# Second MLP product of a decoder layer: operands made ahead in other buffers, the last convolution moved behind them, the residual added by DMA

## The chip, the cores and the metric

One core of a Trainium2 chip runs the whole layer in one launch. The metric is the device time of one execution in microseconds (us). The engines are TensorE (PE, its weight loads PEld), VectorE (DVE), ScalarE (ACT), GpSimd (POOL) and SyncE (SP), which only issues DMAs here.

## The reference, cut to what matters

A hybrid decoder layer (state-space mixer, windowed attention, then a gated MLP) over 1024 positions with 1024 channels, all in float32. The change lies in the last part:

```
up = h @ w_up                                   # 1024 x 5632
up = causal depthwise conv of width 3 (up) + conv_b
val, gate = split(up, 2)                        # 2816 each
x = x + g2 * ((silu(gate) * val) @ w_down)      # second MLP product, then the residual
```

## The kernel before, in words

Everything is held transposed: channels on the partitions, positions along the free axis. The first MLP product makes `up` in 22 tiles f of 128 value and 128 gate channels. Each tile is one 2 by 2 block product done in seven products i = 1 to 7 instead of eight, with sums of operands taken before and of results after. A float32 operand is cut into a high part (fp32r) and the rest (`split`, L137: the high part by ACT through `cpy`, L133, the low part by a subtraction, L118, on DVE or POOL), and `mm3` (L143) makes three matmuls of each pair. After its seven products a tile f has its value half `uv[f]` (buffer H6 or A8) and its gate half `ug[f]` (buffer H7), taken out of PSUM by `took` (L1039). Then `conv` (L1099) runs over the gate into buffer X7 (one ACT instruction at L1100, two DVE instructions at L127), the SiLU follows on ACT, `conv` runs over the value into X6, DVE multiplies both, and SP stores the product to DRAM as `gd[f]` (L1200).

The second MLP product contracts over the 22 tiles, in 11 pairs p cut into three chunks of 3, 4 and 4 pairs (L1153). Again seven products i, in the order 1, 5, 6, 3, 7, 2, 4. A step is one (chunk, i, p), 77 in all, and has 12 matmuls of 128x512. `fetch(p)` loads four tiles of 512 KB (two of `gd`, two of `w_down`) into the buffers `homes[p]`. `operands(i, p)` does up to three DVE subtractions or additions in place (three for i = 5, two for 6, one for 3, 7 and 4), and then two `mixed` calls, each of which takes the next buffer of `SLOTS` and splits the operand into it. `mix_next` does this for the next step in the list; inside the loop it stays three steps ahead (AH, L1223). `put` (L1162) scales a finished bank of PSUM by g2 into the output tile `xo[k]`: by ACT the first time a half tile is written, by DVE (L127) after that.

The operand buffers of the steps come from a cycle of nine: U0, U1, U4, U5, U2, U3, A8, H7, H6. U0 to U5 hold the last weights of the first product, H7 and H6 the last tile's two halves, so step 3 (buffers A8, H7) waits for the last gate convolution and step 4 (H6, U0) for the last value convolution. In the program the last tile's convolutions (f = 21, L1192 to L1200) stand ahead of all but the first two steps' operands.

The residual lies in DRAM as `xd`. At steps 21 and 30 SP loads its eight tiles into H4, H5, X4, X5 (L1231 to L1234), and at eight of the steps 24 to 36 DVE adds a whole 128x1024 tile to `xo[k]` (L1235 to L1237).

The order of the instructions on each engine and queue is laid down when the kernel is built, by a planner that takes the program's order as priority and a simulated timeline for what is ready (L1361). An engine works through its queue in that order. An adding DMA is used once before in this kernel: in `proj` POOL issues 16 of them, 256 KB each (L888), to add the layer's input.

Of the kernel before, what the change touches and what calls it, by code (L numbers as in the profile page):

```python
# [22 lines left out]
FFT = 22  # L23
# [39 lines left out]
def hymba_kernel(ctx, tc, xT, c, wmod, wu, wkvq, small, consts, relb, pq, wglu, wout, wup, wdn, out):  # L63
# [1047 lines left out]
    cn_ = {"slot": 0, "split": 0}  # L1111
# [12 lines left out]
    def mixed(v):  # L1124
        r_ = half(newr(SLOTS[cn_["slot"] % len(SLOTS)]))
        cn_["slot"] += 1
        split(r_, v, "a", "vvp"[cn_["split"] % 3])
        cn_["split"] += 1
        return r_

    SLOTS = ("U0", "U1", "U4", "U5", "U2", "U3", "A8", "H7", "H6")
# [43 lines left out]


# [7 lines left out]
    for n_, (f, i) in enumerate(seq):  # L1184
# [7 lines left out]
        if i == 4:  # L1192
            tg = new("X7")
            conv(tg, FFT + f, ug[f])
            act.activation(out=tg, in_=tg, func=AF.Silu)
        elif i == 3:
            tv = new("X6")
            conv(tv, f, uv[f])
            tt(vec, tv, tv, tg, MUL)
            kept = sync.dma_start(out=gd[f], in_=tv)  # L1200
            if f == 3:
                cact4 = new("H4")
                sync.dma_start(out=cact4, in_=cad.partition_broadcast(128))
            elif 4 <= f < 12:
                with tc.issue_after(kept.ins):
                    emit_mod(36 + f, new("H5"), cact4)
        if f == FFT - 2 and i == 3:
            fetch(0)
            fetch(1)
        if f == FFT - 1 and i == 5:  # L1210
            fetch(2)
        if f == FFT - 1 and i in (4, 3):
            mix_next()
# [3 lines left out]
    xo = [xq[:, k * 1024:(k + 1) * 1024] for k in range(4)] + [new(t_) for t_ in ("W0", "W1", "X6", "X7")]  # L1217
    fetch_at = {5: 3, 8: 4, 12: 5, 16: 6, 24: 7, 28: 8, 33: 9, 46: 10}
    XL = {21: (0, 1, 2, 3), 30: (4, 5, 6, 7)}
    XP = {24: 0, 25: 1, 26: 2, 27: 3, 33: 4, 34: 5, 35: 6, 36: 7}  # L1220
    xt, pend, touched, banks = {}, None, set(), {}
    np_ = 0
    AH = 3  # L1223
    for s_, (c_, i, p) in enumerate(steps):
# [3 lines left out]
        if s_ in fetch_at:  # L1228
            with tc.issue_after(kept.ins):
                fetch(fetch_at[s_])  # L1230
        if s_ in XL:  # L1231
            for k in XL[s_]:
                xt[k] = new(("H4", "H5", "X4", "X5")[k % 4])
                sync.dma_start(out=xt[k], in_=xd[k])  # L1234
        if s_ in XP:  # L1235
            k = XP[s_]
            tt(vec, xo[k], xo[k], xt[k], ADD)  # L1237
# [16 lines left out]
        if p == ps_[1] and pend:  # L1254
            put(*pend)
        if p == ps_[-1]:
# [108 lines left out]
```

## Time and profile before

| | |
|---|---|
| median of 3 runs | 1137.26 us (1137.13 to 1140.05) |
| profiled execution, its own time | 1138.01 us |
| its span, first to last instruction | 1136.1 us |
| mean granted TensorE clock | 0.962 |
| busy: PE, DVE, ACT, POOL | 1050.8, 928.0, 581.0, 269.0 us |
| PE at lines of the chain that ended last | 44% of the span |
| second MLP product, from the first step alone on PE to the end | 903.7 to 1132.4 us |

The profiled execution is 0.75 us longer than the median, and 1.9 us of it lie outside the span. A busy PE says little here, since it is busy in nearly all of the span; what can be changed is seen in the places where it is idle or runs at a lower granted clock (1.00 is 2.4 GHz, 0.50 is 1.2 GHz).

### The profile page before, as it was taken

To read this page: it belongs to the slowest core of one execution; us is meant where nothing else is said; L and a number is where in the kernel's file an instruction comes from. 1 tells how busy PE (TensorE), PEld (TensorE's weight loads), DVE (VectorE), ACT (ScalarE), POOL (GpSimd) and SP (SyncE) were. 2 spreads that over 40 slices of the span, in tenths; PEclk is the share of its full clock that TensorE was granted. 3 is DMA by queue.
4 is the path that set the end of the run, shared out by engine and by line. 5 is a ranking of instruction groups with operands and counts; after the bars stand their busy time and mean duration, and the time that the engine had idled before them with its cause. 6 is when DMAs were issued, how large, how long until landed. Compare 5 with 4: busy or idle time off the path is not lost.

```text
span 1136.1 us, 13319 instructions
## 1 busy us (share of the span) xinstructions
PE 1050.8 (92%) x4692; PEld 828.1 (73%) x4692; DVE 928.0 (82%) x1493; ACT 581.0 (51%) x1008; POOL 269.0 (24%) x153
## 2 busy tenths in 40 slices
PE   6989999579989899779999999999999979989998
PEld 4877777366556577657888888888888768768876
DVE  7994899949887587888777878797778797998985
ACT  5415443578895366736544545455444554434342
POOL 0000000011233102762222223212212143353541
PEclk9989999689999899979999999999999989999999
DMA  9501516014018855222223232423123359220002
GB/s 364 224 19 38 118 50 93 1 66 139 19 47 213 258 180 155 93 93 94 92 86 112 82 128 93 154 88 112 56 93 116 125 210 382 74 93 1 1 38 112
DMA packets 48487, 128.14 MB, mean 113 GB/s; under 512 B 6146, under 2 KB 14114, under 8 KB 48419
## 3 DMA queue, kind: packets, MB, share of 16 engines
q1 hardware_dynamic: 46114, 123.09, 31.8%
q0 software_dynamic: 2304, 4.20, 2.3%
q8 instruction: 37, 0.61, 0.2%
q14 instruction: 32, 0.25, 0.1%
HBM read 105.28 MB, written 21.99 MB: 112 GB/s over the span
## 4 chain that ended last, share of the span: by engine, by line
PE 44%; DVE 11%; ACT 1%; DMA 1%; issue 1%; SPq 0%; DVEq 0%; ACTq 0%
PE bk L97 43%; DVE tA L118 2%; DVE tH L118 2%; DVE tU L118 2%; PE bk L99 1%; DVE tXQ L127 1%; DVE tX L127 1%; DVE tXQ L118 1%; DVE tX L118 1%; DVE tS L118 1%; DMA tS<-in_dram 0%; DMA tX<-xd 0%; ACT tU L133 0%; DVE tHA L118 0%; DMA tW<-in_dram 0%
## 5 line engine op out<-in xcount | busy, mean ns | idle before, releaser
L97 PE MATMUL bk<-tA,tU 128*128 128x512 f32 x516 | 128.1, 395 | 0.8 <-DVE tA L118 0.8
L97 PE MATMUL bk<-tU,tU 128*128 128x512 f32 x516 | 123.4, 391 | 4.8 <-DVE tXQ L127 2.4
L97 PEld LDWEIGHTS bk<-tU,tU 128*128 128x128 f32 x516 | 96.5, 188 | 27.4 <-issue 2.8
L97 PE MATMUL bk<-tH,tU 128*128 128x512 f32 x477 | 115.9, 392 | 0.0
L97 PEld LDWEIGHTS bk<-tA,tU 128*128 128x128 f32 x516 | 96.7, 188 | 24.2 <-DVE tA L118 1.4
L127 DVE SCALAR_TENSOR_TENSOR tX<-tH,sm,tX 128x1023 f32<-128x1023 f32 x66 | 100.2, 1519 | 7.7 <-ACT tX L1100 7.6
L97 PEld LDWEIGHTS bk<-tH,tU 128*128 128x128 f32 x477 | 89.1, 188 | 19.2
L97 PE MATMUL bk<-tA,tXQ 128*128 128x512 f32 x300 | 74.5, 395 | 1.0 <-ACT tH L1053 1.0
L97 PE MATMUL bk<-tH,tA 128*128 128x512 f32 (+1 forms) x168 | 62.5, 502 | 10.6 <-ACT tH L133 6.5
L99 PE MATMUL bk<-tH,tU 128*128 128x512 f32 x267 | 65.8, 402 | 2.3 <-DVE tU L118 2.3
L97 PEld LDWEIGHTS bk<-tA,tXQ 128*128 128x128 f32 x300 | 56.3, 188 | 14.5 <-ACT tH L1053 1.4
L133 ACT CAST tU<-tW 128x512 fp32r<-128x512 f32 (+1 forms) x67 | 47.1, 710 | 38.1 <-PE bk L97 19.9
L118 POOL TENSOR_TENSOR tU<-tW,tU 128x512 fp32r<-128x512 f32 x25 | 36.5, 1467 | 115.1 <-ACT tU L133 93.4
L118 DVE TENSOR_TENSOR tX<-tX,tX 128x512 f32<-128x512 f32 (+1 forms) x63 | 61.6, 982 | 1.7 <-DMA tX<-in_dram 0.9
L118 POOL TENSOR_TENSOR tXQ<-tW,tXQ 128x512 fp32r<-128x512 f32 x12 | 49.8, 4154 | 52.3 <-ACT tXQ L133 32.5
L99 PEld LDWEIGHTS bk<-tH,tU 128*128 128x128 f32 x267 | 51.0, 193 | 15.3 <-DVE tU L118 3.1
L118 POOL TENSOR_TENSOR tH<-tH,att 128x1024 f32<-128x1024 f32 (+1 forms) x9 | 17.0, 1890 | 176.2 <-DVE att L841 149.2
L118 POOL TENSOR_TENSOR tU<-tX,tU 128x512 fp32r<-128x512 f32 x19 | 32.9, 1736 | 85.4 <-ACT tU L133 71.3
L118 DVE TENSOR_TENSOR tU<-tW,tU 128x512 fp32r<-128x512 f32 (+2 forms) x43 | 37.8, 881 | 18.2 <-ACT tU L133 18.2
L97 PE MATMUL bk<-tXQ,tH 128*128 128x256 f32 (+2 forms) x224 | 50.2, 368 | 1.6 <-DVE att L829 1.6
L118 DVE TENSOR_TENSOR tU<-tX,tU 128x512 fp32r<-128x512 f32 x39 | 31.3, 808 | 23.4 <-ACT tU L133 23.4
L97 PEld LDWEIGHTS bk<-tXQ,tH 128*128 128x128 f32 x224 | 44.5, 268 | 8.2 <-DVE att L829 4.3
(351 smaller groups left out, 2423.4 us busy)
## 6 DMA issues: line engine op xcount, KB each, us to landing
tW<-in_dram SPq DMA_DIRECT2D x49, 512.0 KB, 3.3
tX<-in_dram SPq DMA_DIRECT2D x47, 512.0 KB, 3.3
tS<-in_dram SPq DMA_DIRECT2D x30, 512.0 KB, 7.1
gd<-tX SPq DMA_DIRECT2D x22, 512.0 KB, 2.9
tA<-in_dram SPq DMA_DIRECT2D x12, 512.0 KB, 10.0
tH<-in_dram SPq DMA_DIRECT2D x12, 512.0 KB, 5.0
tH<-gd SPq DMA_DIRECT2D x8, 512.0 KB, 4.4
tA<-gd SPq DMA_DIRECT2D x8, 512.0 KB, 9.8
```

Source lines behind the costliest of these rows:

```text
L97: return f(*a, **k)
L99: i = f(*a, **k)
L118: return eng.tensor_tensor(out=o, in0=a, in1=b, op=op)
L127: return vec.scalar_tensor_tensor(out=o, in0=a, scalar=s, in1=b, op0=op0, op1=op1)
L133: act.copy(o, i)
```

## The change

Four edits. (1) The operand buffers of the first five steps are U0, U1 / H12, H13 / H14, H15 / U4, U5 / U2, U3; then comes A8, H7, H6 and the six U in a cycle. H12 to H15 held an operand of product 6 of the first MLP product. Five `mix_next` calls, for steps 0 to 4, stand at the last tile's products 5, 6, 7, 4 and 3 (before: two, at 4 and 3), and `fetch(2)` follows `fetch(0)` and `fetch(1)` at once. (2) The last tile's gate convolution with its SiLU is called at step 2 of the loop, ahead of step 5's operands, and the value convolution, the multiplication and the store at step 3, ahead of step 6's operands. (3) The low parts of the first 12 splits are all DVE's (before: every third was POOL's). (4) The eight residual loads on SP and the eight DVE additions are gone; instead POOL issues 16 adding DMAs of 128x512 (256 KB) from `xd` onto `xo`, four right behind the `put` at each of the steps 22, 26, 30 and 38.

```diff
     def mixed(v):
-        r_ = half(newr(SLOTS[cn_["slot"] % len(SLOTS)]))
-        cn_["slot"] += 1
-        split(r_, v, "a", "vvp"[cn_["split"] % 3])
+        r_ = half(newr(next(SLOTS)))
+        split(r_, v, "a", "vvp"[cn_["split"] % 3] if cn_["split"] >= 12 else "v")
         cn_["split"] += 1
         return r_

-    SLOTS = ("U0", "U1", "U4", "U5", "U2", "U3", "A8", "H7", "H6")
+    SLOTS = itertools.chain(("U0", "U1", "H12", "H13", "H14", "H15", "U4", "U5", "U2", "U3"),
+                            itertools.cycle(("A8", "H7", "H6", "U0", "U1", "U4", "U5", "U2", "U3")))
...
+    kept = {}
+
+    def gate(f):
+        tg = new("X7")
+        conv(tg, FFT + f, ug[f])
+        act.activation(out=tg, in_=tg, func=AF.Silu)
+        return tg
+
+    def value(f, tg):
+        tv = new("X6")
+        conv(tv, f, uv[f])
+        tt(vec, tv, tv, tg, MUL)
+        kept["dma"] = sync.dma_start(out=gd[f], in_=tv)
...
+        if i == 4 and f < FFT - 1:
+            tg = gate(f)
+        elif i == 3 and f < FFT - 1:
+            value(f, tg)
...
         if f == FFT - 2 and i == 3:
-            fetch(0)
-            fetch(1)
-        if f == FFT - 1 and i == 5:
-            fetch(2)
-        if f == FFT - 1 and i in (4, 3):
+            for p in range(3):
+                fetch(p)
+        if f == FFT - 1 and i in (5, 6, 7, 4, 3):
             mix_next()
...
-        if s_ in XL:
-            for k in XL[s_]:
-                xt[k] = new(("H4", "H5", "X4", "X5")[k % 4])
-                sync.dma_start(out=xt[k], in_=xd[k])
-        if s_ in XP:
-            k = XP[s_]
-            tt(vec, xo[k], xo[k], xt[k], ADD)
+        if s_ == 2:
+            tg = gate(FFT - 1)
+        elif s_ == 3:
+            value(FFT - 1, tg)
+            xo += [new(t_) for t_ in ("W0", "W1", "X6", "X7")]
...
         if p == ps_[1] and pend:
             put(*pend)
+            h, dd = DEST[pend[0]]
+            if c_ == 1 and pend[0] in (1, 5, 3, 4) or c_ == 2 and i == 1:
+                for k in range(4 * dd, 4 * dd + 4):
+                    if (k, h) not in added and s_ > 21:
+                        added.add((k, h))
+                        pol.dma_start(out=xo[k][:, h * 512:h * 512 + 512], in_=xd[k][:, h * 512:h * 512 + 512], accum_op=ADD)
```

## Rows read from the trace of the kernel before

**Rows 1.** The timeline of PE where the second product takes over from the first: start us, duration us, engine, line, operation, output and inputs, shape, count, and in brackets the idle time before and what ended it.
```profile
903.68 4.70 PE L97 MATMUL bk<-tU,tU 128*128 128x512 f32 x20
912.84 1.97 PE L97 MATMUL bk<-tH,tA 128*128 128x512 f32 x4 [4.47 <-ACT tH L133]
917.25 3.78 PE L97 MATMUL bk<-tH,tA 128*128 128x512 f32 x8 [2.44 <-DVE tH L118]
920.83 3.11 PE L97 MATMUL bk<-tU,tH 128*128 128x512 f32 x8
923.78 1.08 PE L97 MATMUL bk<-tU,tU 128*128 128x512 f32 x4
```

**Rows 2.** The same timeline a little later, where PE runs without a gap: two starts that are nine steps apart.
```profile
930.14 2.97 PE L97 MATMUL bk<-tA,tU 128*128 128x512 f32 x12
954.85 2.97 PE L97 MATMUL bk<-tA,tU 128*128 128x512 f32 x12
```

**Rows 3.** Windows of the takeover: from:to us, length, busy us and count of PE, PEld, DVE, ACT and POOL, then the granted TensorE clock, the DMA share and GB/s.
```profile
912.84:917.25 4.41, 1.97 (x4) 1.05 (x4) 4.41 (x6) 0.47 (x1) 1.47 (x1) 0.52 0.00 0
917.25:920.83 3.58, 3.58 (x8) 2.81 (x9) 3.58 (x5) 1.16 (x2) 1.05 (x1) 0.50 0.00 0
920.83:923.78 2.95, 2.95 (x9) 2.34 (x8) 1.77 (x4) 1.14 (x2) 2.25 (x1) 0.59 0.56 192
```

**Rows 4.** The timeline of PE after that: every place up to the end where it waited.
```profile
988.71 6.46 PE L97 MATMUL bk<-tU,tU 128*128 128x512 f32 x27 [1.35 <-POOL tU L118]
1000.67 1.89 PE L97 MATMUL bk<-tU,tH 128*128 128x512 f32 x7 [1.54 <-POOL tH L118]
1010.12 2.14 PE L97 MATMUL bk<-tA,tU 128*128 128x512 f32 x8 [0.78 <-DVE tA L118]
1016.50 1.07 PE L97 MATMUL bk<-tU,tU 128*128 128x512 f32 x2 [2.43 <-DVE tXQ L127]
1087.15 2.12 PE L97 MATMUL bk<-tU,tU 128*128 128x512 f32 x8 [0.70 <-DVE tU L118]
```

**Rows 5.** Windows of the second chunk (the first two) and of the third chunk's like stretch, columns as in rows 3.
```profile
960.00:1016.00 56.00, 50.40 (x215) 39.46 (x213) 56.00 (x71) 22.91 (x40) 23.23 (x12) 1.00 0.30 106
1016.00:1045.00 29.00, 28.30 (x121) 22.82 (x122) 23.32 (x35) 11.41 (x20) 11.02 (x7) 1.00 0.10 37
1060.00:1088.00 28.00, 27.30 (x119) 21.73 (x118) 28.00 (x42) 10.98 (x20) 15.99 (x6) 1.00 0.00 1
```

**Rows 6.** The groups of DVE instructions from 963 to 1016 us by shape, those of 128x1024 (the residual additions): line, engine, operation, names, shape, count | busy us, mean ns of one | idle before.
```profile
L118 DVE TENSOR_TENSOR tXQ<-tXQ,tH 128x1024 f32<-128x1024 f32 x2 | 4.0, 1982 | 0.0
L118 DVE TENSOR_TENSOR tX<-tX,tX 128x1024 f32<-128x1024 f32 x2 | 3.4, 1754 | 0.0
L118 DVE TENSOR_TENSOR tXQ<-tXQ,tX 128x1024 f32<-128x1024 f32 x2 | 2.4, 1212 | 0.0
L118 DVE TENSOR_TENSOR tW<-tW,tH 128x1024 f32<-128x1024 f32 x2 | 2.3, 1212 | 0.0
```

**Rows 7.** The timeline of DVE around the takeover: two low parts or convolutions with the idle time before them, the last gate convolution (904.86, 909.49), the last value convolution (913.09, 917.72) and step 3's low part in H7 (916.52).
```profile
883.71 0.69 DVE L118 TENSOR_TENSOR tU<-tH,tU 128x512 fp32r<-128x512 f32 x1 [2.08 <-ACT tU L133]
890.01 1.29 DVE L127 SCALAR_TENSOR_TENSOR tX<-tH,sm,tX 128x1023 f32<-128x1023 f32 x1 [4.16 <-ACT tX L1100]
904.86 2.30 DVE L127 SCALAR_TENSOR_TENSOR tX<-tH,sm,tX 128x1023 f32<-128x1023 f32 x1
909.49 1.27 DVE L127 SCALAR_TENSOR_TENSOR tX<-tH,sm,tX 128x1022 f32<-128x1022 f32 x1
913.09 2.30 DVE L127 SCALAR_TENSOR_TENSOR tX<-tH,sm,tX 128x1023 f32<-128x1023 f32 x1
916.52 0.68 DVE L118 TENSOR_TENSOR tH<-tH,tH 128x512 fp32r<-128x512 f32 x1
917.72 1.27 DVE L127 SCALAR_TENSOR_TENSOR tX<-tH,sm,tX 128x1022 f32<-128x1022 f32 x1
```

**Rows 8.** The timeline of ACT: step 3's high part in H7.
```profile
912.18 0.60 ACT L133 CAST tH<-tH 128x512 fp32r<-128x512 f32 x1
```

**Rows 9.** The timeline of POOL ahead of and in the takeover: the low parts that it made.
```profile
892.63 2.22 POOL L118 TENSOR_TENSOR tU<-tS,tU 128x512 fp32r<-128x512 f32 x1 [26.51 <-ACT tU L133]
904.58 1.50 POOL L118 TENSOR_TENSOR tU<-tA,tU 128x512 fp32r<-128x512 f32 x1 [9.74 <-ACT tU L133]
911.40 2.91 POOL L118 TENSOR_TENSOR tU<-tA,tU 128x512 fp32r<-128x512 f32 x1 [5.31 <-ACT tU L133]
```

**Rows 10.** Line 888, the 16 adding DMAs of the projection: how long POOL was busy with one (min/median/max ns), when, and the time to landing.
```profile
L888 POOL DMA_DIRECT2D tX<-in_dram x8: 860/870/1181, 331.9 to 375.9; - x8
L888 POOL DMA_DIRECT2D tXQ<-in_dram x8: 856/860/865, 369.9 to 430.3; - x8
DMA to landing us min/median/max: 3.6/4.9/8.3
```

**Rows 11.** The window that holds the eight of them onto X4 to X7, columns as in rows 3.
```profile
325.70:376.80 51.10, 48.74 (x204) 31.94 (x203) 37.02 (x81) 32.99 (x78) 16.55 (x13) 0.96 0.68 185
```

**Rows 12.** The timeline of POOL at the start of the first MLP product: its longest instruction.
```profile
467.35 31.91 POOL L118 TENSOR_TENSOR tXQ<-tW,tXQ 128x512 fp32r<-128x512 f32 x1 [4.55 <-DVE tH L127]
```

**Rows 13.** DMA issues: the stores of `gd` (KB each, median us to landing), and the timeline of SP: the first load of `fetch(3)`.
```profile
gd<-tX SPq DMA_DIRECT2D x22, 512.0 KB, 2.9
...
921.77 0.38 SPq L1118 DMA_DIRECT2D tHA<-gd  x1
```

More of the change, by code (lines that the diff above doesn't have):

```diff
@@ L1110, in hymba_kernel @@
              ("H8", "H9", "H10", "H11"), ("S16",), ("A9", "A10", "A11", "A12"), ("H4", "H5", "X4", "X5")]
-    cn_ = {"slot": 0, "split": 0}
+    cn_ = {"split": 0}
     DEST = {1: (0, 0), 2: (0, 0), 3: (1, 0), 6: (1, 0), 5: (1, 1), 7: (1, 1), 4: (0, 1)}
@@ L1191, in hymba_kernel @@
             pst.close()
[L1192 to L1200, printed above, removed]
+        if i == 4 and f < FFT - 1:
+            tg = gate(f)
+        elif i == 3 and f < FFT - 1:
+            value(f, tg)
             if f == 3:
@@ L1204, in hymba_kernel @@
             elif 4 <= f < 12:
-                with tc.issue_after(kept.ins):
+                with tc.issue_after(kept["dma"].ins):
                     emit_mod(36 + f, new("H5"), cact4)
         if f == FFT - 2 and i == 3:
-            fetch(0)
-            fetch(1)
-        if f == FFT - 1 and i == 5:
-            fetch(2)
-        if f == FFT - 1 and i in (4, 3):
+            for p in range(3):
+                fetch(p)
+        if f == FFT - 1 and i in (5, 6, 7, 4, 3):
             mix_next()
     xq = new("XQ")
-    xo = [xq[:, k * 1024:(k + 1) * 1024] for k in range(4)] + [new(t_) for t_ in ("W0", "W1", "X6", "X7")]
+    xo = [xq[:, k * 1024:(k + 1) * 1024] for k in range(4)]
     fetch_at = {5: 3, 8: 4, 12: 5, 16: 6, 24: 7, 28: 8, 33: 9, 46: 10}
-    XL = {21: (0, 1, 2, 3), 30: (4, 5, 6, 7)}
-    XP = {24: 0, 25: 1, 26: 2, 27: 3, 33: 4, 34: 5, 35: 6, 36: 7}
-    xt, pend, touched, banks = {}, None, set(), {}
+    pend, touched, added = None, set(), set()
     np_ = 0
@@ L1228, in hymba_kernel @@
         if s_ in fetch_at:
-            with tc.issue_after(kept.ins):
+            with tc.issue_after(kept["dma"].ins):
                 fetch(fetch_at[s_])
-        if s_ in XL:
-            for k in XL[s_]:
-                xt[k] = new(("H4", "H5", "X4", "X5")[k % 4])
-                sync.dma_start(out=xt[k], in_=xd[k])
-        if s_ in XP:
-            k = XP[s_]
-            tt(vec, xo[k], xo[k], xt[k], ADD)
+        if s_ == 2:
[3 more added lines that the diff above has]
+            xo += [new(t_) for t_ in ("W0", "W1", "X6", "X7")]
         while len(ready) < min(len(steps), s_ + AH + 1):
```

## The prediction
> **What bounds the kernel now.** I read the timeline of PE from the end of the first product on, then the windows for the granted clock, then DVE, ACT and POOL at the places where PE waits. The reader should see three things.
>
> First, the takeover. PE runs 20 matmuls from 903.68, stops for 4.47 us until ACT has step 3's high part in H7, runs 4, and stops for 2.44 us until DVE has the low part [rows 1]. The 16 matmuls after that come slowly: the granted clock, 1.00 before, is 0.50 to 0.59 from 912.84 to 923.78 [rows 3], so at or near the lower level of 1.2 GHz, after the long wait. Undisturbed, nine steps (108 matmuls) take 954.85 - 930.14 = 24.71 us: 2.746 us a step, 0.2288 a matmul [rows 2]. From 903.68 to 923.78 pass 20.10 us for 40 matmuls, worth 9.15 us. **Loss: 10.9 us**, of which 6.9 are idle and 4.0 are the clock and the pipeline's start.
>
> Second, the second chunk. PE waits 1.35, 1.54, 0.78 and 2.43 us [rows 4], and DVE is busy for 56.00 of 56.00 us [rows 5]. Each wait costs some 0.17 us more, since a lone matmul lasts 0.40 us where the next would start after 0.23. **Loss: 6.8 us.** The clock stays at 1.00 [rows 5], also behind the wait of 2.43 us, so such a wait doesn't lower it here.
>
> Third, the third chunk repeats the second without residual additions: DVE is full again (28.00 of 28.00 us), and PE waits once, 0.70 us [rows 4, 5]. **Loss: 0.9 us.** In all 18.6 us from the takeover on; that is the most that the change can give back.
>
> **The five steps made beforehand.** Before, steps 0 to 2 were ready when the first product ended, and step 3 hung on H7. Now steps 3 and 4 have U4, U5, U2, U3, free one by one as the last products end. That is 24 more matmuls, 5.5 us at the undisturbed pace: PE needs step 5 (A8, H7) at 908.4 + 5.5 = 913.9, step 6 (H6, U0) at 916.6. Steps 1 and 2 lie in H12 to H15, free once product 6 of the last tile is through (near 885). DVE was idle for 2.08 us before 883.71 and for 4.16 before 890.01 [rows 7]; their four low parts, 0.68 each, fit there. Before, POOL made one of those at 892.63, taking 2.22 us [rows 9].
>
> **The last convolution.** Nothing is added, but it now has two steps' operands of lower and more of higher priority than before. Step 5 should be in time: the gate convolution's last instruction ended at 909.49 + 1.27 = 910.76 [rows 7], the high part in H7 followed at 912.18 and took 0.60 [rows 8], and DVE made the low part only at 916.52 because the value convolution and subtractions came first. At once it would be done by 913.5, before 913.9. Step 6 is the tight one. The value convolution ended at 917.72 + 1.27 = 918.99 [rows 7]; with 0.60 for the high part and 0.68 for the low one, step 6 would be ready at 920.3, 3.7 us late. What pulls it forward: two convolution instructions took 2.30 us beside POOL's low parts instead of 1.27 [rows 7, 9], and with no POOL work in the first 12 splits that is 2.1 us; two of the low parts of steps 1 and 2, which DVE made after 890, go into its idle time, 1.3 us. What holds it back: of the four low parts that pass from POOL to DVE, two fall into this stretch, 1.4 us. 3.7 - 2.1 - 1.3 + 1.4 = 1.7 us late. I take 1.7 and its 0.17, **1.9 us, in place of 10.9**; the ends are 0 and the unrelieved 3.9, to which the clock's 4.0 would come if that wait were long enough.
>
> **What is moved past other work.** The store of `gd[21]` now goes out behind the later multiplication, and `fetch(3)` behind it on SP. I cost that at nothing: before, `fetch(3)` began at 921.77 [rows 13]; step 21, its first user, is 15 steps or 41 us behind step 6 and is made three steps early, so it has over 30 us. The cover is thinner for X6 and X7: the first `put` into them (product 5's, at step 7) waits until the store has left X6, 2.9 us [rows 13], and product 3 needs its bank two steps (5.5 us) later. Without this cover ACT, which does that `put`, would stand with the next high parts behind it, for 2.9 us at most. `fetch(2)` moves ahead of the last tile's work; nothing waits on it.
>
> **The residual.** Eight DVE additions go: 4.0 + 3.4 + 2.4 + 2.3 = 12.1 us of the full 56 [rows 5, 6]. The waits of that stretch lose 6.8 us, and at each of them the additions already done or under way are worth more than the loss so far. So the stretch should come to what the third chunk shows with the same work and no additions: 0.9 us. Eight loads leave SP; nothing of PE waited on them.
>
> What comes instead is 16 adding DMAs on POOL. Line 888 is the same instruction with the same 256 KB: 0.86 us of POOL, 4.9 us to landing, 8.3 at most [rows 10]. The landing hides: the next `put` on the same half tile is at least eight steps (22 us) behind. On POOL they are 16 x 0.86 = 13.8 us, beside 23.2 + 11.0 = 34.3 busy of 85 [rows 5], so there is room; but they come in fours, 3.4 us in one piece, and each waits for its `put` on DVE while POOL's low parts for coming steps stand behind. The lead of three steps is 8.2 us. Bounds: 0, and all of 13.8 on the path. Near the lower end, since lead and room cover a group; as two of the groups (steps 26, 30) fall where DVE is full and the lead short, I take half of one group, **1.7 us**. So chunk two keeps 0.9 + 1.7 = 2.6 of 6.8.
>
> A page speaks against this edit. The row is that line 888 took 0.86 us with DVE busy for 37.0 of 51.1 us around it [rows 10, 11], not full as it will be here. The Trainium skill's "SBUF — State Buffer" (section "SBUF: two separate sides") says that a DMA issued from GpSimd needs descriptors written by GpSimd, which can't be while VectorE holds the port that they share; by its figure of 3.1 us instead of 0.62 for such a DMA, a group of four would hold POOL for 12.4 us, 4.2 beyond the lead, and the time would be some 1139 us, an estimate from that page. The sum stays with the row of 0.86; what the rows bear out of such a case is rival 4.
>
> **Sum.** Left are 1.9 + 2.6 + 0.9 = 5.4 of 18.6 us: a gain of 13.2. The profiled execution's 1138.01 us becomes 1124.8; it stands 0.75 above the median, so against 1137.26 I predict **1124.0 us**. The case's own range: 1118.7 (nothing left) to 1127.5 (3.9 at the takeover, another group on POOL shown).
>
> **Rivals.**
> 1. *The convolution is the late one.* It lost priority to five steps' operands, and DVE was full from 890 on. If step 6 waits the unrelieved 3.7 us, or steps 5 and 6 share it, and the clock falls as it did after 4.47 us, the takeover keeps 3.9 + 4.0 instead of 1.9: 1130.0 us. For it: DVE's chain is continuous there. Against: its idle 6 us just before.
> 2. *The second chunk stays as it is.* Waits of POOL for DVE's `put`s replace waits for DVE; 6.8 stay instead of 2.6: 1128.2 us. For it: two of the four waits there are on POOL's low parts already [rows 4]. Against: the third chunk.
> 3. *The order does not follow the text.* The planner may issue the last tile and the first steps as before, and only the additions go: 10.9 stay at the takeover, 1133.0 us. Against: it was H7 itself that step 3 waited for, and the buffers do change.
> 4. *Slower: POOL is shut out.* Once POOL's low part took 31.91 us [rows 12] where others take 1.5 to 2.9 [rows 9], while DVE ran on without a gap. If this befalls a low part or a group of DMAs among the DVE's full 56 us, all behind it on POOL is late by 31.9 less the lead of 8.2: 23.7 us, giving 1147.7. It decides from 8.2 + 13.2 + 3.4 = 24.8 us on, since then the gain is gone by more than a measurement can miss. Against: in chunks two and three DVE's `put`s break the run, and line 888 never took more than 1.18 us [rows 10]. The rule of the Trainium skill's "SBUF — State Buffer" named above is of this kind.
>
> **Chances.** Forecast 0.60, rival 1 0.14, rival 2 0.14, rival 3 0.05, rival 4 0.07. A measurement of this kernel can tell about 0.3%, 3.4 us, from no change. The forecast and rivals 1 and 2 are faster by more, rival 3 in two cases of five: 0.90. The rest of rival 3 and a little of rival 4 lie within: 0.04. Slower: 0.06. The range must leave out no more than 2 in 10; it goes from 1118.5 to 1131.0, over rivals 1 and 2, and leaves out 3 and 4.
>
> **What would show it.** Right: PE's timeline goes from the first product through steps 0 to 4 with one wait of 1 to 2 us at most, ended by H6; the clock is 1.00 from 900 to 930; H12 to H15 are written before 890; between 960 and 1016 DVE has idle time, PE waits for under 3 us in all, and POOL shows 16 DMAs of 0.9 us. Wrong: a wait of 4 us or more at step 5 or 6 with a clock near 0.5 behind it (rival 1); PE waiting on POOL's low parts right behind groups of DMAs (rival 2); a POOL instruction of 10 us or more in the second chunk (rival 4).

## The result, and the profile after

The changed kernel's median is 1127.77 us (1125.02 to 1133.07, 8 runs), against 1136.88 us (1133.68 to 1140.05, 8 runs) for the kernel before on the same chip. The ratio is 0.9935, with a 95% interval of 0.9918 to 0.9953: **about 7.4 us faster (5.3 to 9.3)**. The two medians lie 9.1 us apart, inside that interval; the gain is taken from the ratio. The forecast was 13.2.

The profiled execution of the changed kernel took 1126.86 us (span 1125.1). Its span is 11.0 us below that of before, but 3.9 us of this lie ahead of the change: product 4 of tile 20, the same code in both, starts at 885.12 before and at 881.22 after. From there to the last matmul's end pass 247.24 us before and 240.07 after. These 7.2 us agree with the ratio, so I read the traces from there on.

To cut the rest into stretches I use PE groups that recur every nine steps, as in [rows 2], and count each matmul between them at the undisturbed 0.2288 us. What a stretch takes beyond that is its loss.

| stretch | before: from, to | loss | after: from, to | loss |
|---|---|---|---|---|
| takeover (146 matmuls before, 170 after) | 885.12, 930.14 | 11.6 | 881.22, 924.23 | 4.1 |
| second chunk (27 steps, 74.13 undisturbed) | 954.85, 1037.42 | 8.4 | 948.93, 1031.84 | 8.8 |
| third chunk (18 steps, 49.42 undisturbed) | 1062.13, 1112.87 | 1.3 | 1056.55, 1107.42 | 1.45 |

The whole gain, 7.5 us, lies at the takeover. The second chunk, which was to give 4.2, gave nothing. (The recurring groups fall two steps apart in the two kernels: the 27 steps are 16 to 42 before and 18 to 44 after, where the second chunk is 21 to 48. The second chunk's loss is 8.4 here and 6.8 in the prediction because the stretch of 27 steps, not the four waits alone, is measured; the takeover's is 11.6 and not 10.9 because 0.7 us lie ahead of the second product, in both kernels.)

The timeline of PE at the takeover, which answers to [rows 1] (start us, duration us, engine, line, operation, names, shape, count, in brackets the idle time before and what ended it):

```profile
904.35 5.60 PE L97 MATMUL bk<-tU,tU 128*128 128x512 f32 x24
910.09 1.20 PE L97 MATMUL bk<-tH,tA 128*128 128x512 f32 x4
912.40 2.13 PE L97 MATMUL bk<-tH,tA 128*128 128x512 f32 x8 [1.11 <-DVE tH L118]
915.00 2.11 PE L97 MATMUL bk<-tU,tH 128*128 128x512 f32 x8 [0.47 <-ACT tH L133]
917.75 1.19 PE L97 MATMUL bk<-tU,tH 128*128 128x512 f32 x4 [0.64 <-DVE tH L118]
918.78 5.61 PE L97 MATMUL bk<-tU,tU 128*128 128x512 f32 x24
924.23 2.97 PE L97 MATMUL bk<-tA,tU 128*128 128x512 f32 x12
```

Waits of 4.47 and 2.44 us became three of 1.11, 0.47 and 0.64: step 5 for its low part in H7, step 6 for its high and low part in H6. Further on, PE waits here:

```profile
978.75 2.11 PE L97 MATMUL bk<-tH,tH 128*128 128x512 f32 x8 [0.32 <-DVE tH L118]
981.19 2.79 PE L97 MATMUL bk<-tU,tU 128*128 128x512 f32 x11 [0.33 <-DVE tU L118]
984.80 5.06 PE L97 MATMUL bk<-tU,tU 128*128 128x512 f32 x21 [0.82 <-DVE tU L118]
998.41 3.43 PE L97 MATMUL bk<-tU,tH 128*128 128x512 f32 x8 [4.82 <-DVE tU L118]
```

The four waits of [rows 4] in the second chunk (1.35, 1.54, 0.78, 2.43) became four others, the last of them 4.82 us long, and the third chunk's is the same 0.7 (0.69 us, ended at 1076.22). The windows show what the long wait does to the clock (columns as in [rows 3]: from:to, length, busy us and count of PE, PEld, DVE, ACT and POOL, granted clock, DMA share, GB/s):

```profile
904.35:924.23 19.88, 17.52 (x74) 13.21 (x73) 17.43 (x22) 13.82 (x24) 8.82 (x4) 1.00 0.35 124
998.41:1001.70 3.29, 3.29 (x9) 2.65 (x10) 3.29 (x6) 0.00 (x0) 0.00 (x0) 0.56 0.00 0
960.00:1016.00 56.00, 49.71 (x208) 39.45 (x207) 53.24 (x65) 19.98 (x35) 32.93 (x25) 0.97 0.44 67
```

At the takeover the clock now stays at 1.00 (2.4 GHz). Behind the 4.82 us in which PE stood still it is 0.56, near the lower level of 1.2 GHz. The adding DMAs on POOL, the answer to [rows 10] (min/median/max ns, first and last start):

```profile
  L1264 POOL DMA_DIRECT2D tXQ<-xd x8: 862/877/1334, 973.1 to 1012.6; - x8
  L1264 POOL DMA_DIRECT2D tW<-xd x4: 873/1032/1192, 956.8 to 989.5; - x4
  L1264 POOL DMA_DIRECT2D tX<-xd x4: 1314/1534/1861, 957.9 to 991.8; - x4
```

**The first clue.** Every wait of the second chunk in after is on DVE, none on POOL, though eight additions of 12.1 us [rows 6] left DVE. The windows of the 27 steps say why. Before, and then after:

```profile
954.85:1037.42 82.57, 76.27 (x325) 60.29 (x324) 77.44 (x101) 33.19 (x58) 33.62 (x18) 1.00 0.29 101
```

```profile
948.93:1031.84 82.91, 76.62 (x325) 61.55 (x324) 73.47 (x94) 33.22 (x58) 44.42 (x34) 0.98 0.47 106
```

DVE's busy time, the third of the columns, goes from 77.44 us to 73.47: it shed 4.0 of the 12.1 us. The other 8 came back, nearly all as longer instructions: the 93 that are no additions took 65.3 us before, and 94 take 73.47 after. So the theory to test was: **the DMAs cost nothing by themselves, but on POOL's queue they shift POOL's low parts to moments at which these lengthen DVE's instructions.** Rivals were the amount of issue time on POOL, the addition and its landing, the traffic, and a second chunk that is limited without them.

### The profile page after: what moved, and what is told of

The parts are those of the page before. It is cut to its first block, busy times and chain, and to the rows that moved or that the text cites. A ratio compares the mean times of both kernels' runs of the same rounds, so it can differ in the third digit from the quotient of the medians.

```text
span 1125.1 us, 13333 instructions
## 1 busy us (share of the span) xinstructions
PE 1045.2 (93%) x4692; PEld 825.7 (73%) x4692; DVE 923.1 (82%) x1489; ACT 581.7 (52%) x1008; POOL 275.7 (25%) x165
## 4 chain that ended last, share of the span: by engine, by line
PE 46%; DVE 10%; issue 1%; DMA 1%; ACT 1%; POOL 0%; DVEq 0%; ACTq 0%; POOLq 0%
PE bk L97 45%; DVE tH L118 3%; DVE tA L118 2%; DVE tU L118 2%; DVE tX L127 1%; PE bk L99 1%; DMA tX<-in_dram 1%; DVE tX L118 1%; DVE tS L118 1%; DVE tXQ L127 0%; DVE tW L127 0%; DMA tW<-in_dram 0%; DVE tHA L118 0%; DVE tHB L118 0%; POOL tH L118 0%
## 5 line engine op out<-in xcount | busy, mean ns | idle before, releaser
L127 DVE SCALAR_TENSOR_TENSOR tX<-tH,sm,tX 128x1023 f32<-128x1023 f32 x66 | 99.3, 1504 | 3.5 <-ACT tX L1100 3.4
L97 PE MATMUL bk<-tH,tA 128*128 128x512 f32 (+1 forms) x156 | 55.5, 487 | 5.0 <-ACT tH L133 2.1
L118 DVE TENSOR_TENSOR tU<-tX,tU 128x512 fp32r<-128x512 f32 x37 | 28.9, 788 | 23.6 <-ACT tU L133 23.6
```

Of the source, the lines that this page charges most:

```text
L97: return f(*a, **k)
L118: return eng.tensor_tensor(out=o, in0=a, in1=b, op=op)
L127: return vec.scalar_tensor_tensor(out=o, in0=a, scalar=s, in1=b, op0=op0, op1=op1)
```

## The experiments

Each edit is against the changed kernel unless said otherwise; ratios are to the kernel before, on the same chip. "Loss" is measured as in the table.

### The residual left out

```
         if p == ps_[1] and pend:
             put(*pend)
-            h, dd = DEST[pend[0]]
...
-                        pol.dma_start(out=xo[k][...], in_=xd[k][...], accum_op=ADD)
```

> The changed kernel without the residual: neither the 16 adding DMAs nor anything in their place (the layer's residual is left out of the output). Theory A: the adding DMAs are what keeps the second chunk at a loss of 8.8 us, since each makes DVE and POOL instructions beside it longer; without them the loss between the starts of steps 18 and 45 falls to the third chunk's 1.5 us, and the time is 7 us below the changed kernel, some 1120.5. Rival B: the second chunk is bound by its own subtractions and by the head start that DVE lost when PE stopped waiting at the takeover; then the loss stays at 7 to 9 us and the time at 1127 to 1128.

Measured: 1119.22 us, ratio 0.9852 (0.9839 to 0.9866). PE does not wait once in the second chunk; its loss is 0.0. The window of the 27 steps:

```profile
950.24:1024.37 74.13, 74.13 (x325) 60.81 (x324) 66.37 (x94) 33.33 (x58) 34.62 (x18) 1.00 0.15 63
```

The same 94 DVE instructions (one of them stands a few places earlier) take 66.37 us here and 73.47 with the DMAs. So the second chunk is not limited without them: the 16 DMAs cost 8.8 us of PE's time and 7.1 of DVE's.

### The first three parts alone, the residual as before

```
+    XL = {21: (0, 1, 2, 3), 30: (4, 5, 6, 7)}
+    XP = {24: 0, 25: 1, 26: 2, 27: 3, 33: 4, 34: 5, 35: 6, 36: 7}
...
+        if s_ in XP:
+            k = XP[s_]
+            tt(vec, xo[k], xo[k], xt[k], ADD)
...
-                        pol.dma_start(out=xo[k][...], in_=xd[k][...], accum_op=ADD)
```

> The changed kernel with the residual as before (eight loads on SP, eight DVE additions at steps 24 to 36), so edits 1 to 3 alone. Theory A: the takeover keeps its gain of 7.5 us, and the DVE additions lose about what the DMAs lose: 1127 to 1129. Rival B: with a smaller head start the additions (12.1 us of DVE) now come on top of a full DVE: the second chunk loses 15 us or more, time 1134 to 1140, near the kernel before.

Measured: 1126.2 us, ratio 0.9915 (0.9902 to 0.9929); second chunk's loss 7.2, with the additions back on DVE (x101, 75.86 us). The whole change has 0.9935. The intervals overlap, so the residual by DMA adds nothing to the other parts that can be told.

### The residual alone

The kernel before, with the eight loads and additions taken out and the adding DMAs put in.

```
-        if s_ in XP:
-            k = XP[s_]
-            tt(vec, xo[k], xo[k], xt[k], ADD)
...
+                        pol.dma_start(out=xo[k][...], in_=xd[k][...], accum_op=ADD)
```

> The kernel before with the residual by 16 adding DMAs alone (edit 4). Theory A: the DMAs cost the second chunk what the additions did, so 1135 to 1138, no change. Rival B: with DVE's head start kept, the removed additions pay: the chunk's loss falls from 8.4 to about 2 us, time 1130 to 1131.

Measured: 1135.38 us, ratio 1.000 (0.9989 to 1.0011). The takeover's waits are 4.42 and 2.34 us, as in [rows 1]; the second chunk loses 9.6, with a wait of 4.24 us for DVE at 1004.23. This part by itself is worth nothing.

### The DMAs written late, at steps 40 to 46

```
-            h, dd = DEST[pend[0]]
-            if c_ == 1 and pend[0] in (1, 5, 3, 4) or c_ == 2 and i == 1:
...
+        for hh, d_ in {40: ((1, 0),), 42: ((0, 0),), 44: ((1, 1),), 46: ((0, 1),)}.get(s_, ()):
+            for k in range(4 * d_, 4 * d_ + 4):
+                pol.dma_start(out=xo[k][...], in_=xd[k][...], accum_op=ADD)
```

> The changed kernel with the same 16 adding DMAs issued at steps 40, 42, 44 and 46, four each, where DVE was busy for only 18.9 of 28.3 us. Theory A: beside an idle DVE they cost nothing, the second chunk's loss falls to 1.5 us and the time to 1120 to 1122. Rival B: the loss stays at 7 to 9 us, 1127 to 1128.

Measured: 1119.21 us, ratio 0.9858 (0.9843 to 0.9874); second chunk's loss 2.5. The text moved further than the instructions: the planner still issued two groups at 956.0 to 960.8 and 972.4 to 978.5, where they are in the changed kernel too, and waits of 0.32, 0.30 and 0.82 us stay. The other two groups went to 1002.7 and 1013.0, and the wait of 4.82 us is gone. So most of the cost hangs on the one group that the changed kernel issues at 988.9.

### The DMAs behind the last put on the same half tile

```
-            if c_ == 1 and pend[0] in (1, 5, 3, 4) or c_ == 2 and i == 1:
+            if c_ == 1 and pend[0] in (3, 7, 2) or c_ == 2 and i == 1:
```

> The changed kernel with each group of four adding DMAs behind a put of the same half tiles that comes later in the second chunk (steps 38, 42, 46, 50), so that no group can be issued beside the full DVE of steps 21 to 36; in the run with the late DMAs two groups had still been issued there, since nothing held them back, and 2.5 us of loss stayed. Theory A (a group costs only beside a full DVE): the second chunk's loss falls to 0 to 0.5 us and the time is 2 us below that run, 1116.5 to 1118. Rival: the group at step 50 now lies at the start of the third chunk's full stretch and moves the loss there: 1119 to 1122.

Measured: 1118.99 us, ratio 0.9848 (0.9824 to 0.9871). Second chunk's loss 0.0, with all 16 DMAs still on POOL. Nine of them lie in the stretch of 27 steps (POOL 42.03 us busy, DVE 66.76 us), the other seven behind it, up to 1044.40, and PE does not wait there either. The third chunk's first nine steps took 27.37 us and lost 2.66 where the kernel without a residual lost 1.3:

```profile
1055.91 3.72 PE L97 MATMUL bk<-tU,tU 128*128 128x512 f32 x15 [0.60 <-POOL tU L118]
```

Waits of 0.18 and 0.65 us for DVE follow. Both theories had a part: most of the cost went with the place, and some 1.4 us came back later. The 0.60 is a low part of POOL that took 5.76 us from 1050.10 on, where it took 5.17 in the changed kernel.

### Twice as many DMAs of half the size

```
-                        pol.dma_start(out=xo[k][:, h * 512:h * 512 + 512], ...)
+                        for q in (h * 512, h * 512 + 256):
+                            pol.dma_start(out=xo[k][:, q:q + 256], ...)
```

> The changed kernel with every adding DMA cut into two of 128x256 at the same place: 32 issues, the same bytes. Theory A1 (the cost is the issue on POOL, 0.86 us each whatever the bytes): the second chunk's loss rises from 8.8 to 13 to 18 us, time 1132 to 1137. Rival A2 (the cost goes with the bytes added in SBUF): loss 8 to 10 us, time 1127 to 1129.

Measured: 1125.93 us, ratio 0.9915 (0.9897 to 0.9933); second chunk's loss 8.45. POOL was busy 56.05 us instead of 44.42, one issue taking 0.87 to 3.5 us, and PE lost no more, though its longest wait, now 3.50 us, lies at another place, ended at 982.49. The cost does not grow with the number of issues or with POOL's busy time, so the first theory missed.

### Plain stores on POOL in place of the additions

The same places, bytes and waits; the residual is left out.

```
-                        pol.dma_start(out=xo[k][...], in_=xd[k][...], accum_op=ADD)
+                        pol.dma_start(out=xd[k][...], in_=xo[k][...])
```

> The changed kernel with 16 plain DMAs on POOL's queue in the places of the adding ones: each stores the same half tile from xo to xd, waits for the same put and moves 256 KB, but adds nothing (the residual is left out). DVE's order is the changed kernel's. Theory A1 (issue on POOL): the loss of the second chunk stays at 7 to 9 us, time 1126 to 1128. Rival A2 (the addition itself, which reads and writes SBUF): the loss falls under 2 us, time 1119 to 1121.

Measured: 1124.46 us, ratio 0.9897 (0.9875 to 0.9918); second chunk's loss 7.0:

```profile
949.82:1030.92 81.10, 76.79 (x326) 61.66 (x324) 72.08 (x94) 33.23 (x58) 35.77 (x34) 0.98 0.27 109
```

An issue takes 0.54 us here, and POOL is busy 35.77 us, only 1.2 more than without any DMA. The 16 issues take 8.9 of that, so POOL's 18 low parts, 34.6 us without any DMA, take only some 27 here, while DVE takes 72.08 us instead of 66.37: POOL's instructions, which had room, got shorter, and DVE's, which had none, got longer. PE loses most of what the additions cost, 7.0 of 8.8 us, so most of the cost is not the addition.

### The same stores on SP

```
-                        pol.dma_start(out=xo[k][...], in_=xd[k][...], accum_op=ADD)
+                        sync.dma_start(out=xd[k][...], in_=xo[k][...])
```

> The same 16 plain stores issued by SP instead of POOL (the residual is left out). Theory A1: no issue on POOL, so the second chunk loses under 1 us, time 1119 to 1120, as without any residual. Rival: if the traffic of these DMAs or the wait of later puts for them is what costs, the loss stays at 5 us or more, time 1124 to 1128.

Measured: 1118.79 us, ratio 0.9854 (0.9834 to 0.9874); second chunk's loss 0.0:

```profile
949.00:1023.14 74.14, 74.14 (x326) 60.82 (x324) 66.36 (x94) 33.33 (x58) 34.55 (x18) 1.00 0.30 119
```

The same traffic as with the stores on POOL, with the same waits for the `put`s, is free on the other queue: DVE takes 66.36 us, as without any DMA. So for the stores traffic and the later `put`s' waits for the transfers are out, and the place is POOL's queue. Adding DMAs were not tried on another queue.

### The last convolution in its old place

The kernel with the DMAs behind the last put, the convolution undone:

```
-        if i == 4 and f < FFT - 1:
+        if i == 4:
             tg = gate(f)
-        elif i == 3 and f < FFT - 1:
+        elif i == 3:
             value(f, tg)
...
-        if s_ == 2:
-            tg = gate(FFT - 1)
-        elif s_ == 3:
-            value(FFT - 1, tg)
```

> The kernel with the DMAs behind a later put (chunk two's loss is 0 there), but the last tile's two convolutions in their old place ahead of the steps' operands, so the takeover has the other buffers and the DVE-only low parts without the moved convolution. Theory A: the other buffers give the gain, the convolution's place little; H7 and H6 come free some 2 us earlier, the three waits at steps 5 and 6 (2.2 us) shrink to 1 us or go, time 1117 to 1119. Rival B: the early convolution pushes the operands of steps 3 and 4 back on the full DVE, a new wait of 2 to 5 us comes ahead of step 5, time 1120 to 1123.

Measured: 1118.56 us, ratio 0.9846 (0.9825 to 0.9868). By their names the instructions stand in the same order on every engine as with the convolution moved, and the takeover's waits are the same but for 0.02 us: 1.12, 0.46 and 0.62. Moving the convolution in the text changes nothing, because the planner does not follow the text here. Both expectations of other waits missed.

### A third of the first low parts on POOL again

The kernel with the DMAs behind the last put, and:

```
-        split(r_, v, "a", "vvp"[cn_["split"] % 3] if cn_["split"] >= 12 else "v")
+        split(r_, v, "a", "vvp"[cn_["split"] % 3])
```

> The same kernel (DMAs behind a later put, convolution moved) with the low parts of every third of the first 12 splits on POOL again. Theory A: POOL's low parts lengthen DVE's instructions beside them (2.30 instead of 1.27 us before), so DVE gains nothing by giving four away: waits at the takeover of 2 to 4 us, time 1118 to 1121. Rival B: DVE is only relieved by 2.4 us, and the waits at steps 5 and 6 go: 1116.5 to 1118.

Measured: 1119.83 us, ratio 0.9851 (0.9829 to 0.9874), which can't be told from the kernel it was made from. In the trace the takeover took 43.76 us instead of 43.00. Its waits, 0.29, 1.16, 0.32 and 1.33, sum to 3.1 instead of 2.2 us, and one of them ends on POOL:

```profile
913.17 2.13 PE L97 MATMUL bk<-tH,tA 128*128 128x512 f32 x8 [1.16 <-POOL tH L118]
```

So of the 7.5 us at the takeover some 0.8 are the low parts' move to DVE (from two traces alone), none the convolution's, and the rest, 6.7, by difference, the other buffers, with the operands of three more steps made ahead in them; these were not undone by themselves.

### The wait alone

In place of each DMA POOL copies one column of the same tile, so that it waits for the same `put` and then has little to do; the residual is left out.

```
-                        pol.dma_start(out=xo[k][...], in_=xd[k][...], accum_op=ADD)
+                        pol.tensor_copy(out=mods[:, len(added) - 1:len(added)],
+                                        in_=xo[k][:, h * 512:h * 512 + 1])
```

> The changed kernel with each of the 16 adding DMAs replaced by a POOL copy of one column from the same half tile of xo (the residual is left out): at the same place of POOL's queue, with the same wait for DVE's put, but no issue and no transfer; DVE's order is the changed kernel's but for one swap. Theory W (POOL's wait for DVE's put holds back the low parts behind it, which then take DVE's time): the second chunk keeps 5 to 9 us of its 8.8 us loss, time 1124 to 1128. Theory I (the time that POOL spends issuing is what costs): the loss falls under 2 us, time 1118 to 1121.

Measured: 1124.42 us, ratio 0.9896 (0.9876 to 0.9916); second chunk's loss 4.1, between what the two theories said:

```profile
949.57:1027.84 78.27, 75.00 (x325) 60.63 (x324) 70.11 (x93) 33.23 (x58) 35.94 (x34) 1.00 0.15 59
```

PE's waits there are 0.31, 0.34 and 2.62 us. The copies are not quite nothing: each holds POOL for 0.18 to 0.66 us, 8.2 us in all, about what the 16 plain stores' issues take (8.9). So the row of losses, 0 with the stores on SP, 4.1 with the copies, 7.0 with the plain stores, 8.8 with the adding DMAs, shows that no DMA is needed for about half of the loss: a wait for the `put` on POOL's queue with a short instruction behind it makes that much. It does not tell the wait from the time behind it.

### All four groups behind the last puts, none in the third chunk

```
-            if c_ == 1 and pend[0] in (1, 5, 3, 4) or c_ == 2 and i == 1:
+            if c_ == 1 and pend[0] in (3, 7, 2):
...
+                if pend[0] == 7:
+                    with tc.issue_after(grp.ins):
+                        for k in range(4, 8):
+                            pol.dma_start(out=xo[k][:, 0:512], in_=xd[k][:, 0:512], accum_op=ADD)
```

> The adding DMAs at steps 38, 42 and 46 behind those puts, and the fourth group held directly behind the group of step 42 in POOL's queue instead of at step 50. Theory A: no group lies beside a full DVE, neither in the second nor in the third chunk; the second chunk loses 0, the third 1.4 instead of 2.7 us: 1116.5 to 1118. Rival: eight DMAs in one piece hold POOL for 7 us, past the lead of the low parts, and a wait of 1 to 3 us comes at steps 43 to 46: 1119 to 1121.

Measured: 1119.71 us, ratio 0.9852 (0.9829 to 0.9875). Second chunk's loss 0.0; nine steps of the third took 26.83 us and lost 2.1, with waits of 0.39 us for POOL, 0.19 and 0.64, although the last DMA's issue now ends at 1027.75, 19 us ahead of these steps, and not 4.7 us as before. So the last group's place was not what the third chunk lost by. The first theory missed, and the rival was right in the time alone: the wait that it had at steps 43 to 46 did not come.

## Why: one group of DMAs read row by row

The largest loss, the wait of 4.82 us, ends at 998.41 on a low part of DVE. DVE up to there, in the changed kernel (timeline, columns as before):

```profile
987.68 1.40 DVE L127 SCALAR_TENSOR_TENSOR tW<-bk,mod,tW 128x512 f32<-128x512 f32 x2
989.00 1.39 DVE L127 SCALAR_TENSOR_TENSOR tX<-bk,mod,tX 128x512 f32<-128x512 f32 x2
990.32 4.11 DVE L118 TENSOR_TENSOR tA<-tA,tA 128x512 f32<-128x512 f32 x2
994.34 1.74 DVE L118 TENSOR_TENSOR tH<-tHB,tH 128x512 fp32r<-128x512 f32 x1
996.01 0.68 DVE L118 TENSOR_TENSOR tA<-tA,tA 128x512 f32<-128x512 f32 x1
996.61 1.75 DVE L118 TENSOR_TENSOR tU<-tHA,tU 128x512 fp32r<-128x512 f32 x1
```

and the same instructions with the residual left out:

```profile
986.44 1.39 DVE L127 SCALAR_TENSOR_TENSOR tW<-bk,mod,tW 128x512 f32<-128x512 f32 x2
987.76 1.39 DVE L127 SCALAR_TENSOR_TENSOR tX<-bk,mod,tX 128x512 f32<-128x512 f32 x2
989.08 1.27 DVE L118 TENSOR_TENSOR tA<-tA,tA 128x512 f32<-128x512 f32 x2
990.28 0.67 DVE L118 TENSOR_TENSOR tH<-tHB,tH 128x512 fp32r<-128x512 f32 x1
990.89 0.67 DVE L118 TENSOR_TENSOR tA<-tA,tA 128x512 f32<-128x512 f32 x1
991.49 0.67 DVE L118 TENSOR_TENSOR tU<-tHA,tU 128x512 fp32r<-128x512 f32 x1
```

The four `put`s (L127) read a PSUM bank and take the same time in both. The four rows behind them, down to the low part in tU that PE waits for, are the same five instructions, and take 8.04 us (990.32 to 998.36) in the one and 3.08 (989.08 to 992.16) in the other: 5.0 us more, about as long as the wait. What POOL did meanwhile, in the changed kernel:

```profile
984.35 4.57 POOL L118 TENSOR_TENSOR tH<-tA,tH 128x512 fp32r<-128x512 f32 x1 [3.77 <-ACT tH L133]
988.86 1.78 POOL L1264 DMA_DIRECT2D tW<-xd  x2
990.01 1.95 POOL L118 TENSOR_TENSOR tU<-tH,tU 128x512 fp32r<-128x512 f32 x1
991.25 2.45 POOL L1264 DMA_DIRECT2D tX<-xd  x2
992.40 3.12 POOL L118 TENSOR_TENSOR tU<-tA,tU 128x512 fp32r<-128x512 f32 x1
996.24 1.56 POOL L118 TENSOR_TENSOR tH<-tHB,tH 128x512 fp32r<-128x512 f32 x1 [0.72 <-ACT tH L133]
```

and without the DMAs:

```profile
983.11 4.58 POOL L118 TENSOR_TENSOR tH<-tA,tH 128x512 fp32r<-128x512 f32 x1 [4.37 <-ACT tH L133]
987.64 1.29 POOL L118 TENSOR_TENSOR tU<-tH,tU 128x512 fp32r<-128x512 f32 x1
989.60 4.92 POOL L118 TENSOR_TENSOR tU<-tA,tU 128x512 fp32r<-128x512 f32 x1 [0.67 <-ACT tU L133]
```

In both kernels POOL ends its first low part some 1.25 us after the `put`s begin (988.92 and 987.69). Without the DMAs the next low part starts at once and ends at 988.93, still within the `put`s, which end at 989.15; the subtraction in tA then runs at its usual pace. With them, two DMAs come first. The low part starts at 990.01, 0.4 us ahead of the end of the `put`s, and runs into DVE's subtractions, two of which take 4.11 instead of 1.27 us. Then two more DMAs, and the next low parts start at 992.40 and 996.24, beside DVE instructions of 1.74 and 1.75 us instead of 0.67.

So in this group the time in which DVE reads PSUM is the time in which POOL's low part costs it nothing, and the two DMAs onto tW take it up with 1.1 us of issue. They did not have to wait for the `put`s: POOL has no idle time ahead of them, and in the whole chunk only 2.1 us of its idle time end on a `put`. Through the second low part without the DMAs (4.92 us, from 989.60) DVE runs on undisturbed: there POOL was the one that waited. Why POOL waits in that case and DVE in the others is not settled; in the case shown the low part was under way when DVE's first subtraction began, in the other it started half a microsecond behind it.

The Trainium skill's "SBUF — State Buffer" (section "SBUF: two separate sides") says that a VectorE operation with two SBUF inputs and a GpSimd operation that reads SBUF hold a shared pair of ports in turn, the one that "starts first" for its whole instruction. The two cases shown agree with it in who waits, with 4.11 instead of 1.27 us on DVE in the one and 4.92 instead of 1.29 on POOL in the other. In the second POOL waited longer than for one instruction: the low part ends at 994.52, 1.2 us behind the start of DVE's next `put` (993.30), so DVE's subtractions from 989.60 up to there seem to have gone ahead of it, one behind the other.

Two other runs have the same group. With the plain stores and with the copies POOL did wait for the `put` on tW (first three rows: stores, last three: copies):

```profile
989.62 1.20 POOL L1264 DMA_DIRECT2D xd<-tW  x2 [3.92 <-DVE tW L127]
991.22 4.11 DVE L118 TENSOR_TENSOR tA<-tA,tA 128x512 f32<-128x512 f32 x2
996.46 0.68 DVE L118 TENSOR_TENSOR tU<-tHA,tU 128x512 fp32r<-128x512 f32 x1
988.47 0.18 POOL L1264 COPY mods<-tW 128x1 f32<-128x1 f32 x1 [3.68 <-DVE tW L127]
990.30 1.42 DVE L118 TENSOR_TENSOR tA<-tA,tA 128x512 f32<-128x512 f32 x2
993.95 1.75 DVE L118 TENSOR_TENSOR tU<-tHA,tU 128x512 fp32r<-128x512 f32 x1
```

PE's wait at this place follows the same five DVE instructions in all four runs:

| run | five DVE instructions, us | more than without DMAs | PE's wait behind them |
|---|---|---|---|
| no residual | 3.08 | | none |
| copies | 5.40 | 2.3 | 2.62 |
| plain stores on POOL | 5.92 | 2.8 | 3.15 |
| changed kernel | 8.04 | 5.0 | 4.82 |

The issues alone do not lengthen DVE's instructions: in the first group of the changed kernel POOL issues from 956.75 on, and DVE's subtractions at 957.28 and 957.88 keep 0.68 us; the next long one, 2.21 us from 959.08, runs beside a low part of POOL (958.71).

```profile
956.75 1.77 POOL L1264 DMA_DIRECT2D tW<-xd  x2
957.28 0.68 DVE L118 TENSOR_TENSOR tHA<-tHA 128x512 f32<-128x512 f32 x1
```

Of the 7.1 us that DVE's 94 instructions take more than without the residual, 5.0 are the five above. The other 2.1 come in the group before. There two DVE instructions took 1.86 us (975.57) and 2.52 (978.62) beside low parts of POOL that DMAs had pushed back (975.25 and 978.96); without the DMAs they took 0.67 and 0.68. Two others got 0.4 shorter each. The waits of 0.32 and 0.33 us end on these instructions or on the one between them; that of 0.82 comes a few DVE instructions later.

## Why the prediction was right or wrong, point by point

**Direction and range: right, the range by its width.** Faster, and 1127.77 lies between 1118.5 and 1131.0, but the gain is 7.4 of the 13.2 us foretold. The time is in the range because that was drawn over rivals 1 and 2; the case's own range ended at 1127.5 (its terms, 2.0 more at the takeover and 1.7 more for the DMAs, make 1127.7). Of the 13.2 us, 1.5 are missing at the takeover (3.4 left instead of 1.9) and 4.6 in the second chunk (0.4 lost where 4.2 were to be gained).

**The five steps made beforehand: right.** PE reached step 5 at 910.09, which is 914.0 on the clock of before (3.9 us later), where 913.9 was foretold. The low parts in H12 to H15 were made by DVE at 884.4, 885.6, 887.4 and 894.6 on that clock, all but one ahead of 890. The buffers, with the operands made ahead in them, give some 6.7 us of the gain, by difference.

**The last convolution: late by more, and not where foretold.** Measured as in the prediction, from the second product's start, 3.4 us are left where 1.9 were foretold: from 904.35 to 924.23 pass 19.88 us for 72 matmuls, worth 16.47. The late one was not step 6 alone, which waited 0.47 and 0.64 us. Step 5 was to have its low part in time, and waited 1.11 us for it, so that the two shared the lateness as rival 1 had it:

```profile
906.42 1.28 DVE L127 SCALAR_TENSOR_TENSOR tX<-tH,sm,tX 128x1022 f32<-128x1022 f32 x1
...
908.22 2.32 DVE L127 SCALAR_TENSOR_TENSOR tX<-tH,sm,tX 128x1023 f32<-128x1023 f32 x1
...
911.67 0.68 DVE L118 TENSOR_TENSOR tH<-tA,tH 128x512 fp32r<-128x512 f32 x1
912.27 1.27 DVE L127 SCALAR_TENSOR_TENSOR tX<-tH,sm,tX 128x1022 f32<-128x1022 f32 x1
```

The low part in H7 (911.67) was not made at once behind the gate convolution but behind the first half of the value convolution. That half still took 2.32 us and not the relieved 1.27: a low part of POOL ran beside it from 907.22 for 2.24 us, since POOL's share begins again behind the first 12 splits, and the first of it came this early. The clock stayed at 1.00, as the forecast had it and rival 1 did not. And the part "moved behind them" was none: the order of the instructions did not change with it, so rival 3's idea was true of this one part.

**The residual: wrong, and this is the step that failed.** "So the stretch should come to what the third chunk shows with the same work and no additions: 0.9 us" counted 12.1 us of additions as gone from DVE, and "1.7 us" for the DMAs counted room on POOL. The stretch lost 8.8 where 8.4 less 4.2 were foretold (by the prediction's measure, the waits with 0.17 each, 7.0 instead of 2.6, and 1.3 more by the clock). Taking the additions out is worth what I thought and more (loss 0.0 without any residual), and POOL had the room: the halved DMAs filled 11.6 us more of it at no more loss. What I had not priced is that POOL's low parts, pushed back by the DMAs ahead of them on its queue, make DVE's own instructions longer: 7.1 us for the same 94. The rows of before had such a pair: a convolution on DVE of 2.30 us instead of 1.27 beside a low part of POOL [rows 7, 9]. I used it as a relief at the takeover and not as a price in the second chunk. Of the signs of being right, DVE has its idle time between 960 and 1016 (53.24 of 56.00 us busy) and the 16 DMAs are there, but PE waits for 6.3 us where under 3 were foretold.

**Rival 2** came true in its outcome (second chunk as it was, 1128.2 foretold), and its cause in part at most: the cost does come by POOL's queue, but POOL waited for the `put`s on DVE for only 2.1 us, and not at the costliest group. Its sign did not come: I had looked for PE waiting on POOL's low parts, and PE waited on DVE's. **Rival 4** did not come: the longest low part on POOL in the second chunk of the changed kernel took 4.57 us.

**The Trainium skill's figure weighed there.** The issues took 0.86 to 1.86 us, though DVE was busy for 53.24 of 56.00 us in the window above. So the estimate of some 1139 us did not come true, and the row of 0.86 was nearer, if low. It was worked out from the 3.1 us in the Trainium skill's "SBUF — State Buffer", section "SBUF: two separate sides", which stand there for a DMA beside a DVE `tensor_copy`; DVE's work here was another.

**Moved past other work: nothing, as foretold.** `fetch(3)` on SP now begins at 916.93, 0.9 us earlier on the same clock than before [rows 13], and no wait of PE follows from it.

**Left open.** Where the 1.4 us in the third chunk come from with the DMAs late is not known; 0.9 of them stayed when the last DMA was issued 19 us ahead. Nor is it known how much of the second chunk's loss is the wait for a `put` and how much the time that the DMA then holds POOL, or why the adding DMAs cost 1.8 us more than plain stores. Whether a DMA of POOL that needs no wait would be free was not tried, since the addition must follow a `put`.

**A better version.** With the DMAs behind the last put, one changed line, the kernel takes 1118.99 us: 1.5% below the kernel before (ratio 0.9848, 0.9824 to 0.9871), and its interval lies wholly below that of the change (0.9918 to 0.9953). The versions with the DMAs written late, with the convolution undone, or with the four groups joined can't be told from it.

## What to carry to other kernels

Work taken off a full engine comes off its busy time only if the work that replaces it does not make that engine's other instructions longer: compare the engine's busy time for the same count of instructions, not its list. A DMA costs its queue the wait for its data as well as its issue, and everything behind it on that queue shifts; so put it on a queue with nothing urgent behind it, or at a place where the data has long been ready. When a stretch stops short of the foretold gain, leave the new work out altogether first, then put a stand-in with the same wait in its place, then move it to another queue: the first gives the price of the work, the third that of the queue. The second gives the price of the wait only if the stand-in holds the queue for much less time than the work, which the copies here did not.

## What the runs showed of the hardware that was not expected

- A DVE subtraction of 128x512 took 0.60 us from start to start, and 1.7 when a low part of POOL ran beside it; DVE's reads of PSUM kept their 0.66 us beside POOL.
- An adding DMA of 256 KB held POOL for 0.86 to 1.86 us, a plain store of the same size for 0.54 to 0.61; one of half the size for 0.87 to 3.5.
- PE's clock after a wait: 0.56 after 4.82 us, 0.50 behind a wait of 4.24 us (the residual alone), 0.53 behind 3.50 us (halved DMAs), 0.65 behind 3.15 us (stores on POOL), but 1.00 behind 2.62 us (the wait alone). Of the 8.8 us that the second chunk lost, some 1.3 are this: eight matmuls from 998.41 on took 3.27 us to the next group's start instead of 1.83, and 0.17 of the difference come with any wait.
